# A hybrid diffusion layer on one core: three modulation blocks move to the vector engine in operations of 1024 columns, and the output product adds two row blocks in PSUM

## Chip, cores and metric

The kernel runs on one core of a Trainium2 chip. The metric is the device time of one execution in microseconds, here the median of several runs. Engines have the short names of the profile: PE (TensorE, matmuls), PEld (its weight loads), DVE (VectorE), ACT (ScalarE), POOL (GpSimd), SP (SyncE, which issues the weight transfers). Each engine works through its own list of instructions strictly in order, so an instruction that waits holds up all that stand behind it on its engine.

## What is computed

One layer with a gated short convolution as token mixer and a mixture of 16 experts; 256 tokens, 2048 channels, all in float32. Cut to what matters here:

```python
mod = split(silu(c) @ mod_w + mod_b, 6)            # six rows of 2048; mod_w is 2048 x 12288
h = x * (1 + mod[1]) + mod[0]
gate_b, gate_c, val = split(h @ w_in, 3)           # w_in is 2048 x 6144
o = (gate_b * depthwise_conv3(gate_c * val)) @ w_out
x = layer_norm(ALPHA * x + mod[2] * o)
h2 = x * (1 + mod[4]) + mod[3]                     # goes to the router and the experts
x = layer_norm(ALPHA * x + mod[5] * hier_moe(h2))  # top 1 of 4 groups, top 2 of its 4 experts
```

Each of the six `mod` rows is a product of one vector of 2048 with a 2048 x 2048 block of weights: 16 MB are read for very little arithmetic.

## The kernel before, in words

All weights are read once, as a stream of loads of up to 1.5 MB in a fixed order (`steps`, line 564 on). A load goes into one of six places of a ring (`get`, line 118) and is issued by SP when the instructions that used the place's former tenant are done. The part up to the router, which the change touches, runs like this:

- **Input product** (`cin_step`, line 390). The weights `w_in` are cut into eight groups of channels. The first four groups are worked through in five passes over the contraction (`acc_step`, line 442: passes `i` = 0 to 4, each adding to sums in SBUF, `acc`), because the rows of `mod[0]` and `mod[1]` that `h` needs come in only pass by pass. The last four groups (`full_steps`, line 453) accumulate in PSUM over four steps of one load each. A step has three splits of 1024 columns (`split`, line 376): ACT rounds the weights to `hic` (line 379), DVE subtracts to get the rest `loc` (line 380), and PE multiplies three products of these pieces with the pieces of `h` (lines 387 to 389), 24 matmuls of 256 columns for a split. There are two buffers each for `hic` and `loc`: ACT's next rounding waits until PE is through with the split before last.
- **Convolution** (`conv_group`, line 415) of a group once its sums are complete: six DVE operations and two of ACT, ending in `yh` and `yl`.
- **Output product** (`cout_step`, line 506): 16 steps of 512 rows (`qt`) by 512 columns (`j`), each with two splits (`hio`, `loo`) and 24 matmuls of 512 columns. Each of the 16 adds its own result to the residual: DVE multiplies it by `mod[2]` (line 531), and DVE (`qt` 0 and 3) or POOL (`qt` 1 and 2, line 535) adds it to `xt`.
- **Modulation.** `mod[0]`, `mod[1]`, `mod[2]` and three eighths of `mod[3]` and `mod[4]` are multiplied on PE, with the weights as moving columns, in four partitions' quarters (lines 258 and 285). The other five quarters of `mod[3]` and `mod[4]` (`ON_V`) go to DVE: 15 operations of 512 columns each (line 263), which `gemv_cols` puts into a `queue`; each `split` takes two of them off the queue behind its own subtraction.

DVE's list is therefore a mixture of subtractions, for which PE waits, and of queued multiplications, which nobody waits for until the block is complete. After the last output step come the layer norm's statistics (lines 538 and 637), the router and the sixteen experts, which read 302 MB of weights and are not touched by the change.

Of the kernel before, what the change touches and what calls it, by code (L numbers as in the profile page):

```python
# [19 lines left out]
P = 128  # L20
D = 2048
# [12 lines left out]
EXTRA = [0, 1, 0, 0, 12]  # L34
# [16 lines left out]
# Pieces of the columns of the down product; those of the last experts end with smaller ones.  # L51
# [14 lines left out]
def trunk_kernel(  # L66
# [36 lines left out]
    # ---------------------------------------------------------------- weight stream  # L103
# [14 lines left out]
    def get(i):  # L118
        """the tile of load i, whose predecessors have been used; issues what now has a place"""
# [24 lines left out]
    def expert_loads(e, pieces=QUARTERS):  # L144
        """loads of an expert's gate and up weights, and of its down weights by pieces of the columns"""
# [19 lines left out]
    # ---------------------------------------------------------------- constants, small inputs  # L165
# [10 lines left out]
    # picks rows 0, 32, 64 and 96  # L176
# [38 lines left out]
    # arithmetic that waits for its turn on the tensor engine, and on the vector engine  # L215
# [10 lines left out]
    def gemv_cols(m, c0, n, on_vector=False):  # L226
# [3 lines left out]
        nb, k0 = n // P, c0 // P  # L230

        def late():
            pt = aux_tile(f"gc{m}_{c0}")
            for i in range(nb):
                TE.transpose(pt[:, i * P : (i + 1) * P], box["r"][:, i * P : (i + 1) * P], ident)
# [999 lines left out]
```

## Time and profile before

| what | value |
|---|---|
| median of 3 runs | 1348.4 us (1347.04 to 1348.72) |
| profiled execution, span from first to last instruction | 1343.3 us; the page gives no other time of it, and the median is 5.1 us above it |
| PE busy | 1190.9 us (89%) |
| DVE busy | 724.2 us (54%) |
| ACT busy | 404.6 us (30%) |
| POOL busy | 30.3 us (2%) |
| transfers | 475.85 MB, mean 354 GB/s |

Busy is the time in which at least one instruction of an engine ran. A matmul's end is modelled and later than the start of the next one, so PE's pace is read from the distance of starts in the timeline, not from a duration. Of float32 matmuls two records stand in the trace for one in the program. [...]

### The profile page before, as it was taken

What the parts mean: (1) busy time and instruction counts of PE and PEld (TensorE: products, weight loads), DVE (VectorE), ACT (ScalarE), POOL (GpSimd) and SP (SyncE); (2) the same over time, 40 slices, a digit from 0 to 9 for tenths busy, and PEclk for the clock granted to TensorE, in tenths of its full rate; (3) what the DMA queues carried; (4) which work ended last, traced back from release to release, by engine and by line L of the source; (5) the groups of instructions that cost most, each with busy time, mean ns of one, the idle gap of its engine ahead of it and who ended that gap; (6) DMA issues with size and microseconds to landing.
All of it is one profiled execution on the core that took longest, in us unless ns stands there. A gap on an engine that the chain in (4) does not pass through costs nothing. (4 is left out here: it accounts for less than half of the span.)

```text
span 1343.3 us, 23490 instructions
## 1 busy us (share of the span) xinstructions
PE 1190.9 (89%) x9429; PEld 856.0 (64%) x9429; DVE 724.2 (54%) x1526; ACT 404.6 (30%) x795; POOL 30.3 (2%) x60
## 2 busy tenths in 40 slices
PE   4999999999999999998789878997689888898883
PEld 2778876978699875775367446774267454554553
DVE  2665565597789878686266434583147321122217
ACT  1333333434244334563035223451026110100020
POOL 0000000000400120000000000000000000000000
PEclk7999999999999999999889899998789899999996
DMA  9999879799989879979999899989999999999992
GB/s 321 354 396 395 298 279 398 276 310 351 357 312 337 296 280 342 364 263 365 413 414 347 316 414 411 400 304 381 412 412 393 336 412 412 413 371 414 412 410 78
DMA packets 240947, 475.85 MB, mean 354 GB/s; under 512 B 10968, under 2 KB 74680, under 8 KB 240576
## 3 DMA queue, kind: packets, MB, share of 16 engines
q1 hardware_dynamic: 235808, 471.88, 93.2%
q10 hardware_dynamic: 5024, 2.40, 0.6%
q8 instruction: 76, 1.25, 0.3%
q14 instruction: 39, 0.32, 0.1%
HBM read 472.16 MB, written 2.10 MB: 353 GB/s over the span
## 5 line engine op out<-in xcount | busy, mean ns | idle before, releaser
L904 PE MATMUL gue<-w,xgp 128*32 128x384 f32 (+1 forms) x1536 | 218.1, 554 | 71.2 <-DMA w<-in_ex_w_up_dram 59.0
L387 PE MATMUL ci<-hhi,hic 128*128 128x256 f32 x768 | 221.1, 289 | 2.7 <-ACT hic L379 1.4
L389 PE MATMUL ci<-hhi,loc 128*128 128x256 f32 x768 | 218.6, 286 | 3.6 <-DVE loc L380 3.5
L388 PE MATMUL ci<-hlo,hic 128*128 128x256 f32 x768 | 217.9, 284 | 0.8 <-DVE hlo L374 0.7
L904 PEld LDWEIGHTS gue<-w,xgp 128*32 128x32 f32 (+1 forms) x1536 | 83.1, 130 | 197.8 <-issue 83.0
L693 DVE TENSOR_TENSOR parts<-w,parts 128x256 fp32r<-128x256 f32 (+1 forms) x320 | 135.3, 475 | 73.2 <-ACT parts L692 70.4
L692 ACT CAST parts<-w 128x256 fp32r<-128x256 f32 (+1 forms) x320 | 131.3, 449 | 114.5 <-PE gue L901 72.7
L379 ACT CAST hic<-w 128x1024 fp32r<-128x1024 f32 (+1 forms) x108 | 102.5, 954 | 183.2 <-PE ci L388 159.0
L387 PEld LDWEIGHTS ci<-hhi,hic 128*128 128x128 f32 x768 | 145.1, 189 | 14.9 <-issue 8.4
L389 PEld LDWEIGHTS ci<-hhi,loc 128*128 128x128 f32 x768 | 145.2, 190 | 9.5 <-DVE loc L380 6.0
L388 PEld LDWEIGHTS ci<-hlo,hic 128*128 128x128 f32 x768 | 146.4, 191 | 5.6 <-DVE hlo L374 2.5
L380 DVE TENSOR_TENSOR loc<-w,hic 128x1024 fp32r<-128x1024 f32 (+1 forms) x108 | 118.7, 1108 | 35.2 <-ACT hic L379 35.0
L921 ACT COPY gse<-gue 128x384 f32<-128x384 f32 x16 | 7.7, 480 | 314.8 <-PE gue L904 314.8
L904 PE MATMUL gue<-w,xfp 128*128 128x384 f32 x256 | 93.9, 498 | 2.5 <-DMA w<-in_ex_w_gate_dram 2.5
L1014 DVE TENSOR_TENSOR Y<-dne,m 32x128 f32<-32x128 f32 (+2 forms) x176 | 52.6, 299 | 42.3 <-PE dne L947 39.3
L448 DVE TENSOR_TENSOR acc<-acc,ci 128x512 f32<-128x512 f32 x48 | 33.0, 687 | 60.4 <-PE ci L389 60.4
L822 PE MATMUL gap<-ohp,xt 128*128 128x128 f32 x512 | 63.6, 279 | 1.7 <-DVE xtp L837 1.0
L822 PEld LDWEIGHTS gap<-ohp,xt 128*128 128x128 f32 x512 | 59.5, 192 | 8.7 <-issue 4.2
L258 PE MATMUL gv<-w,sT 128*32 128x512 f32 (+1 forms) x416 | 57.6, 569 | 8.2 <-DMA w<-in_mod_w_dram 8.2
L904 PEld LDWEIGHTS gue<-w,xfp 128*128 128x128 f32 x256 | 48.3, 194 | 23.5 <-issue 3.9
L263 DVE SCALAR_TENSOR_TENSOR rows<-w,sT,rows 128x512 f32<-128x512 f32 x75 | 57.9, 773 | 1.3
L954 PE MATMUL dne<-parts,ahe 128*128 128x256 f32 x192 | 57.6, 300 | 0.3 <-DVE parts L693 0.2
(302 smaller groups left out, 1679.8 us busy)
## 6 DMA issues: line engine op xcount, KB each, us to landing
w<-in_ex_w_gate_dram SPq DMA_DIRECT2D x64, 1536.0 KB, 13.6
w<-in_ex_w_up_dram SPq DMA_DIRECT2D x64, 1536.0 KB, 15.6
w<-in_ex_w_down_dram SPq DMA_DIRECT2D x60, 1536.0 KB, 15.0
w<-in_mod_w_dram SPq DMA_DIRECT2D x48, 1536.0 KB, 9.3
w<-in_conv_in_w_dram SPq DMA_DIRECT2D x84, 512.0 KB, 6.9
w<-in_mod_w_dram SPq DMA_DIRECT2D x22, 1024.0 KB, 8.0
w<-in_conv_out_w_dram SPq DMA_DIRECT2D x16, 1024.0 KB, 6.9
w<-in_conv_in_w_dram SPq DMA_DIRECT2D x24, 256.0 KB, 7.2
```

Of the source, the lines that this page charges most:

```text
L258: TE.matmul(box["ps"][32 * g : 32 * g + 32, :n], sT[:, kt : kt + 1].to_broadcast([P, 32]), ws, start=kt < 4, stop=kt >= 12)
L263: V.scalar_tensor_tensor(out=box["r"][:, :n], in0=ws, scalar=sT[:, kt : kt + 1], in1=box["r"][:, :n], op0=ALU.mult, op1=ALU.add)
L379: S.copy(hi[:, :n], src)
L380: V.tensor_sub(lo[:, :n], src, hi[:, :n].bitcast(F32))
L387: TE.matmul(ps, whi, ahi, start=start, stop=False)
L388: TE.matmul(ps, whi, alo, start=False, stop=False)
L389: TE.matmul(ps, wlo, ahi, start=False, stop=stop)
L692: S.copy(hi[:, :n], src)
L693: V.tensor_sub(lo[:, :n], src, hi[:, :n].bitcast(F32))
L822: TE.matmul(ps[:, k * n : (k + 1) * n], xn[:, h, (k0 + k) * P : (k0 + k + 1) * P], oh[:, h, :n], start=h == 0, stop=h == 1)
L904: TE.matmul(dst, big[0][:, KF.index(kt), :] if cc == 128 else xg[:, kt, :cc], src, start=st_, stop=sp_)
L954: TE.matmul(o, a[i], lo[:, :256], start=False, stop=sp_ and m == 1)
```

## The change

`mod[2]`, `mod[3]` and `mod[4]` are multiplied on DVE as a whole, in six halves of 1024 columns: one ACT multiplication and 15 DVE operations of 1024 columns for a half. Their loads are blocks of 3 x 128 rows by 1024 columns. Each `split` takes one queued operation, or two when more than three are queued. Each half's sums over partitions come from eight small products with a column of ones (`col_sums`), instead of transposes and a reduction; for `mod[2]` from two products with ones of 512 columns (`mod2_rows`). Three of the loads now stand in pass 3 and eight in pass 4 (`EXTRA`); the rest stand between the later steps.

The output product runs over pairs of row blocks: `qt` 0 and 1 (then 2 and 3) accumulate in one pair of PSUM tiles, so the multiplication by `mod[2]` and the addition to `xt` happen 8 times instead of 16, and POOL adds nothing any more. The first half of the product stands in one block of eight steps behind the second step of group 4, after a flush of the queue; the second half stands at the end. Two things move from DVE to ACT: the unrounded `h` (line 373) and the copies of pass 0 (line 446).

```diff
-EXTRA = [0, 1, 0, 0, 12]
+EXTRA = [0, 1, 0, 3, 8]
-VN = 2
-ON_V = [[0, 1, 0, 1], [0, 1, 1, 1]]
+WIDE = 1024
...
+    def col_sums(m, c0, n, rows_, ones_):
+        pt, nb, k0 = aux_tile(f"gc{m}_{c0}"), n // P, c0 // P
+        for i in range(nb):
+            TE.matmul(pt[:, i : i + 1], rows_[:, i * P : (i + 1) * P], ones_, start=True, stop=True)
+        V.scalar_tensor_tensor(
+            out=modT[:, m, k0 : k0 + nb], in0=pt[:, :nb], scalar=1.0 if m in (1, 4) else 0.0,
+            in1=modbT[:, m * KT + k0 : m * KT + k0 + nb], op0=ALU.add, op1=ALU.add)
...
+    def gemv_vector(m, c0, done):
+        box = {}
+        per = 3072 // WIDE
+        for t0 in range(0, KT, per):
+            nt = min(per, KT - t0)
+            def work(w, t0=t0, nt=nt):
+                for k in range(nt):
+                    kt = t0 + k
+                    ws = w[:, k * WIDE : (k + 1) * WIDE]
+                    if kt == 0:
+                        box["r"] = mod2b[:, c0 : c0 + WIDE] if m == 2 else big_tile(f"rows{m}{c0}")[:, :WIDE]
+                        S.mul(box["r"], ws, sT[:, kt : kt + 1])
+                        continue
+                    def fn(ws=ws, kt=kt):
+                        V.scalar_tensor_tensor(out=box["r"], in0=ws, scalar=sT[:, kt : kt + 1], in1=box["r"],
+                                               op0=ALU.mult, op1=ALU.add)
+                        if kt == KT - 1:
+                            pending.append(lambda: done(box["r"]))
+                    queue.append(fn)
+            yield mod_load(m, c0, WIDE, t0, nt), work
...
+    def mod2_rows(c0, r):
+        for i in range(WIDE // 512):
+            q = c0 // 512 + i
+            rq, o = r[:, i * 512 : (i + 1) * 512], slice(32 * q, 32 * q + 32)
+            V.tensor_tensor(out=rq[o], in0=rq[o], in1=bias_rows[2][o], op=ALU.add)
+            ps = aux_tile(f"gb2{q}")
+            TE.matmul(ps[:, :], onesF.to_broadcast([P, P]), rq, start=True, stop=True)
+            S.copy(mod2b[:, q * 512 : (q + 1) * 512], ps[:, :])
...
-                V.tensor_scalar(out=ht, in0=src, scalar1=sc, scalar2=sh, op0=ALU.mult, op1=ALU.add)
+                S.activation(ht, src, AF.Identity, bias=sh, scale=sc)
...
-        for fn in queue[:VN]:
-            fn()
-        del queue[:VN]
+        drain(2 if len(queue) > 3 else 1)
...
-                    V.tensor_copy(accs[g][:, a, :], pss[a][:, :])
+                    S.copy(accs[g][:, a, :], pss[a][:, :])
...
+    def cout_steps(half):
+        out = []
+        for j in range(4):
+            pso = []
+            for qt in (2 * half, 2 * half + 1):
...
+                def work(w, qt=qt, j=j, pso=pso):
+                    if qt % 2 == 0:
+                        pso.extend(mm_tile(f"co{half}{j}{h}") for h in range(2))
...
+                                first, last = (qt % 2, pr, k) == (0, 0, 0), (qt % 2, pr, k) == (1, 1, 1)
+                                TE.matmul(pso[h][:, :], yh[:, k, a:b], wh, start=first, stop=False)
+                                TE.matmul(pso[h][:, :], yl[:, k, a:b], wh, start=False, stop=False)
+                                TE.matmul(pso[h][:, :], yh[:, k, a:b], wl, start=False, stop=last)
+                    if qt % 2 == 0:
+                        return
...
-                elif qt < 3:
-                    G.tensor_tensor(out=xs, in0=xs, in1=tmp, op=ALU.add)
...
-        if g < 6:
-            rest += fs[:2] + qt + fs[2:]
-        elif g == 6:
-            rest += fs
-        else:
-            rest += fs + qt_last
+        if g == ACC_GROUPS:
+            fs = fs[:2] + [(None, lambda w: flush())] + cout_steps(0) + fs[2:]
+        rest += fs
```

What the scheduler makes of it on DVE is seen at three places. In the rows, `loc_GA` and `loo` are the subtractions of a split (G the group, A the split), `acc` the additions of a pass, `mod2b` and `rows` the sums of a modulation block, `t` the multiplication by `mod[2]`, `x3` three instructions of the kind in a row.

DVE in pass 3, between the splits of group 2 and of group 3, before:

```order
L380 TENSOR_TENSOR loc_22_1674<-w_1472,hic_22_1673 128x1024
L448 TENSOR_TENSOR acc_185<-acc_185,ci_21_1615 128x512
L448 TENSOR_TENSOR acc_185<-acc_185,ci_22_1616 128x512
L380 TENSOR_TENSOR loc_30_1726<-w_1583,hic_30_1725 128x1024
L380 TENSOR_TENSOR loc_31_1754<-w_1583,hic_31_1753 128x1024
```

and now:

```order
L470 TENSOR_TENSOR acc_185<-acc_185,ci_21_1609 128x512
L275 SCALAR_TENSOR_TENSOR mod2b<-w_1479,sT,mod2b 128x1024 x2
L470 TENSOR_TENSOR acc_185<-acc_185,ci_22_1610 128x512
L275 SCALAR_TENSOR_TENSOR mod2b<-w_1479,sT,mod2b 128x1024
L275 SCALAR_TENSOR_TENSOR mod2b<-w_1577,sT,mod2b 128x1024 x3
L275 SCALAR_TENSOR_TENSOR mod2b<-w_1586,sT,mod2b 128x1024 x3
L404 TENSOR_TENSOR loc_30_1718<-w_1594,hic_30_1717 128x1024
L404 TENSOR_TENSOR loc_31_1748<-w_1594,hic_31_1747 128x1024
```

The flush ahead of the next pass puts nine multiplications between two subtractions that stood two additions apart.

DVE in the first half of the output product, before:

```order
L380 TENSOR_TENSOR loo_2736<-w_2617,hio_2735 128x1024
L531 TENSOR_TENSOR t_2721<-co_2683,mod2b 128x512
L531 TENSOR_TENSOR t_2724<-co_2684,mod2b 128x512
L533 SCALAR_TENSOR_TENSOR xt<-xt,t_2721 128x512
L533 SCALAR_TENSOR_TENSOR xt<-xt,t_2724 128x512
L263 SCALAR_TENSOR_TENSOR rows_2679<-w_2481,sT,rows_2679 128x512
L380 TENSOR_TENSOR loo_2754<-w_2617,hio_2753 128x1024
```

and now:

```order
L404 TENSOR_TENSOR loo_2718<-w_2596,hio_2717 128x1024
L275 SCALAR_TENSOR_TENSOR rows_2681<-w_2594,sT,rows_2681 128x1024
L275 SCALAR_TENSOR_TENSOR rows_2681<-w_2635,sT,rows_2681 128x1024 x3
L404 TENSOR_TENSOR loo_2739<-w_2637,hio_2738 128x1024
L404 TENSOR_TENSOR loo_2757<-w_2637,hio_2756 128x1024
L275 SCALAR_TENSOR_TENSOR rows_2681<-w_2679,sT,rows_2681 128x1024 x2
L561 TENSOR_TENSOR t_2773<-co_2697,mod2b 128x512
```

Up to four wide multiplications stand between two pairs of subtractions.

DVE between groups 4 and 5, now:

```order
L404 TENSOR_TENSOR loc_52_3150<-w_2869,hic_52_3149 128x1024
L453 TENSOR_TENSOR v_3070<-v_3070,ci_40_2314 128x512
L275 SCALAR_TENSOR_TENSOR rows_2964<-w_2873,sT,rows_2964 128x1024
L457 TENSOR_TENSOR yl_3079<-v_3070,yh_3078 128x512
L275 SCALAR_TENSOR_TENSOR rows_2964<-w_2873,sT,rows_2964 128x1024 x2
L275 SCALAR_TENSOR_TENSOR rows_2964<-w_2962,sT,rows_2964 128x1024 x2
L404 TENSOR_TENSOR loc_50_3187<-w_2976,hic_50_3186 128x1024
```

Five wide multiplications and two operations of the convolution stand between two subtractions here; before, the same two had one operation of the convolution between them.

## Rows read from the trace of the kernel before

**Rows 1.** Busy time of each engine in stretches of 25 us; the first line names the columns.

```profile
core 0: us, PE busy (x) PEld busy (x) DVE busy (x) ACT busy (x) POOL busy (x), PEclk, DMA share, GB/s
...
400.00:425.00 25.00, 24.75 (x206) 24.54 (x206) 23.62 (x32) 11.10 (x13) 0.00 (x0) 1.00 0.98 352
...
650.00:675.00 25.00, 17.18 (x182) 8.93 (x176) 3.14 (x11) 2.88 (x8) 0.00 (x0) 0.86 1.04 412
...
950.00:975.00 25.00, 16.32 (x189) 6.73 (x181) 4.50 (x18) 1.30 (x4) 0.00 (x0) 0.80 1.04 411
```

**Rows 2.** The same for three longer stretches up to the router.

```profile
165.00:250.00 85.00, 80.58 (x617) 61.50 (x616) 54.19 (x79) 31.57 (x43) 0.00 (x0) 1.00 0.94 347
250.00:450.00 200.00, 196.85 (x1415) 174.19 (x1414) 161.30 (x199) 76.50 (x84) 13.52 (x8) 1.00 0.90 314
450.00:513.00 63.00, 61.06 (x309) 42.24 (x311) 50.21 (x72) 20.66 (x24) 13.40 (x8) 1.00 0.82 294
```

**Rows 3.** DVE's and ACT's lists near 427 us: start, duration, engine, line, tiles, count.

```profile
426.35 1.53 DVE L263 SCALAR_TENSOR_TENSOR rows<-w,sT,rows 128x512 f32<-128x512 f32 x2
...
427.00 1.05 ACT L379 CAST hic<-w 128x1024 fp32r<-128x1024 f32 x1 [1.21 <-PE ci L388]
...
429.88 1.05 ACT L379 CAST hic<-w 128x1024 fp32r<-128x1024 f32 x1 [1.83 <-PE ci L388]
```

**Rows 4.** ACT's list in the output product.

```profile
478.62 1.05 ACT L379 CAST hio<-w 128x1024 fp32r<-128x1024 f32 x1 [1.67 <-PE co L525]
481.34 1.05 ACT L379 CAST hio<-w 128x1024 fp32r<-128x1024 f32 x1 [1.67 <-PE co L525]
```

**Rows 5.** Groups of instructions up to 520 us: count, busy us, mean ns, idle time before.

```profile
L380 DVE TENSOR_TENSOR loc<-w,hic 128x1024 fp32r<-128x1024 f32 x84 | 102.7, 1228 | 30.6 <-ACT hic L379 30.4
...
L263 DVE SCALAR_TENSOR_TENSOR rows<-w,sT,rows 128x512 f32<-128x512 f32 x75 | 57.9, 773 | 1.3
...
L258 PE MATMUL gv<-w,sT 128*32 128x512 f32 x288 | 44.4, 599 | 0.0
L380 DVE TENSOR_TENSOR loo<-w,hio 128x1024 fp32r<-128x1024 f32 x32 | 41.9, 1313 | 15.4 <-ACT hio L379 15.3
L285 PE MATMUL gv<-w,sT 128*32 128x512 f32 x230 | 34.0, 596 | 0.0
...
L535 POOL TENSOR_TENSOR xt<-xt,t 128x512 f32<-128x512 f32 x16 | 26.9, 1704 | 451.5 <-DVE t L531 451.5
...
L531 DVE TENSOR_TENSOR t<-co,mod2b 128x512 f32<-128x512 f32 x32 | 21.4, 687 | 2.7 <-PE co L525 2.4 <-PE lps L501 0.2
L380 DVE TENSOR_TENSOR loc<-w,hic 128x512 fp32r<-128x512 f32 x24 | 16.0, 686 | 4.6 <-ACT hic L379 4.6
...
L235 PE MATMUL gc<-ident,rows 128*128 128x128 f32 x64 | 10.5, 282 | 0.5 <-ACT rows L270 0.5
L371 ACT ACTIVATE hhi<-xT,modT 128x256 fp32r<-128x256 f32 x16 | 9.0, 564 | 9.9 <-DVE ht L373 5.6 <-PE xT L366 2.3 <-DVE modT L239 2.0
```

**Rows 6.** The experts' gather products, from the same view of the whole span.

```profile
L822 PE MATMUL gap<-ohp,xt 128*128 128x128 f32 x512 | 63.6, 279 | 1.7 <-DVE xtp L837 1.0 <-DVE xgp L790 0.7
```

**Rows 7.** DVE's list: pass 3, a convolution, the first step of group 4, the layer norm.

```profile
164.75 0.69 DVE L448 TENSOR_TENSOR acc<-acc,ci 128x512 f32<-128x512 f32 x1 [3.88 <-PE ci L389]
...
246.12 0.69 DVE L420 TENSOR_TENSOR u<-acc 128x512 f32<-128x512 f32 x1
246.73 1.22 DVE L380 TENSOR_TENSOR loc<-w,hic 128x1024 fp32r<-128x1024 f32 x1
247.86 0.88 DVE L426 SCALAR_TENSOR_TENSOR v<-u,T2t,v 128x255 f32<-128x255 f32 x2
...
249.44 1.22 DVE L380 TENSOR_TENSOR loc<-w,hic 128x1024 fp32r<-128x1024 f32 x1
...
512.59 0.38 DVE L637 BATCH_NORM_AGGREGATE mv<-stats 128x2 f32<-128x24 f32 x2
```

**Rows 8.** The input product's matmuls: count, shortest, median and longest, first and last start.

```profile
L387 PE MATMUL ci<-hhi,hic x768: 274/282/684, 27.8 to 450.0; 128*128 128x256 f32 x192
```

More of the change, by code (lines that the diff above doesn't have):

```diff
@@ L248, in work @@
                 if t0 == 0:
[L249 to L252 removed]
+                    box["ps"] = aux_tile(f"gv{m}_{c0}")
                 for k in range(nt):
@@ L268, in work @@
-                if t0 + nt == KT and not on_vector:
-                    box["r"] = p1.tile([P, 512], F32, tag="rows", bufs=2, name=f"rows{m}{c0}")
-                    S.copy(box["r"][:, :n], box["ps"][:, :n])
-                    pending.append(late)
-            yield mod_load(m, c0, n, t0, nt), work
+                    TE.matmul(box["ps"][32 * g : 32 * g + 32, :n], sT[:, kt : kt + 1].to_broadcast([P, 32]),
+                              w[:, k * n : (k + 1) * n], start=kt < 4, stop=kt >= 12)
@@ L372, in make_h, with drain @@
                 ht = p1.tile([P, T], F32, tag="e", bufs=3, name=f"ht{kt}")
-                V.tensor_scalar(out=ht, in0=src, scalar1=sc, scalar2=sh, op0=ALU.mult, op1=ALU.add)
+                S.activation(ht, src, AF.Identity, bias=sh, scale=sc)
                 V.tensor_sub(hlo[:, kt, :], ht, hhi[:, kt, :].bitcast(F32))
+    def drain(n):
+        for fn in queue[:n]:
+            fn()
+        del queue[:n]
     def split(src, n, name):
@@ new lines, in cout_steps, with load @@
+    def cout_steps(half):
[3 more added lines that the diff above has]
+            for qt in (2 * half, 2 * half + 1):
+                def load(w, qt=qt, j=j):
+                    nc.sync.dma_start(
+                        w[:, :2048].rearrange("p (t c) -> p t c", c=512),
+                        rows(cout[qt * 512 : (qt + 1) * 512, j * 512 : (j + 1) * 512]),
+                    )
+                def work(w, qt=qt, j=j, pso=pso):
+                    if qt % 2 == 0:
+                        pso.extend(mm_tile(f"co{half}{j}{h}") for h in range(2))
+                    for pr in range(2):
+                        hi, lo = split(w[:, pr * 1024 : (pr + 1) * 1024], 1024, f"o{qt}{j}{pr}")
+                        yh, yl = yhi[qt * 2 + pr], ylo[qt * 2 + pr]
+                        for k in range(2):
+                            for h in range(2):
+                                a, b = h * P, (h + 1) * P
+                                wh, wl = hi[:, k * 512 : (k + 1) * 512], lo[:, k * 512 : (k + 1) * 512]
+                                first, last = (qt % 2, pr, k) == (0, 0, 0), (qt % 2, pr, k) == (1, 1, 1)
[4 more added lines that the diff above has]
+                        return
+                    if half and j > 0:
+                        router_part(j - 1)
+                    for h in range(2):
+                        xs = xt[:, h, j * 512 : (j + 1) * 512]
+                        tmp = p1.tile([P, 512], F32, tag="e", bufs=3, name=f"t{half}{j}{h}")
+                        V.tensor_mul(tmp, pso[h][:, :], mod2b[:, j * 512 : (j + 1) * 512])
+                        if half == 0:
+                            V.scalar_tensor_tensor(out=xs, in0=xs, scalar=ALPHA, in1=tmp, op0=ALU.mult, op1=ALU.add)
+                        else:
+                            V.tensor_add(xs, xs, tmp)
+                            V.bn_stats(stats[:, h, j, :], xs)
+                    if half and j == 3:
+                        router_part(3)
+                out.append((load, work))
+        return out
@@ L587, in trunk_kernel @@
     steps = h_mods(0) + [(None, lambda w: h_hook(0)())]
-    late = [st for m in (2, 3, 4) for q in range(4) for st in mods(m, q)]
+    late = [st for m in (2, 3, 4) for q in range(D // WIDE) for st in mods(m, q)]
     last = [st for q in range(4) for st in mods(5, q)]
```

76 lines of the change are left out of this document (9 added, 67 removed).

## Prediction, made before the changed kernel was run

> **What bounds the kernel now.** I began with the busy times by stretches, since the change ends where the router begins. From 165 to 450 us PE is busy all but 7.6 of 285 us, at the full granted clock; DVE is at 64% and then at 81%, and the transfers keep a share of 0.94 and 0.90 [rows 2]. So up to the router the kernel hangs on PE. Later stretches, among the experts, look different: there the transfers run at 1.04 and PE waits [rows 1]; whatever happens ahead of them shifts them as a whole, because at the router the transfers have slack already (0.82) [rows 2].
>
> Next comes PE's pace. ACT's roundings of an input product's splits start 2.88 us apart where nothing disturbs [rows 3]; that is 24 matmuls at 0.12 us. In the output product they start 2.72 us apart [rows 4]. Within such a beat DVE has one subtraction (next start 1.13 us later [rows 7]) and two queued multiplications of 512 columns (1.53 us [rows 3]): 2.66 of 2.88 us. It fits, barely: from 400 to 425 us DVE is busy 23.6 of 25 us, PE 24.75 [rows 1]. The reader should see that DVE is the second engine at its limit, not a free one.
>
> **The change, part by part.**
>
> *PE loses work.* `mod[2]` had 64 products, 128 records at 34.0 / 230 = 0.148 us: 18.9 us. The three PE quarters of `mod[3]` and `mod[4]` had 48, 96 records at 44.4 / 288 = 0.154 us: 14.8 us [rows 5]. The transposes for sums (32 at 10.5 / 64 = 0.164 us, 5.2 us [rows 5]) become 32 one-column products; bounds are the transpose's 0.164 and a 128-column product's two records, 2 x 63.6 / 512 = 0.25 us [rows 6]. I take 0.25, so +2.8 us. In all PE loses 31 us.
>
> *DVE gains work.* 75 operations of 512 columns become 90 of 1024; 88 of them come after 165 us. No wide one is in the trace. Below it is bounded by the narrow one, 0.77 us, above by two, 1.55 us [rows 5]. The subtraction of the same operand kinds grows from 0.686 to 1.228 us when its columns double [rows 5], so 0.773 + 0.542 = 1.31 us lone and, with the overlap to a neighbour seen in the lists, 1.28 us. That is 113 us for 88 where 58 us stood. The 16 dropped multiplications by `mod[2]` give back 16 x 0.6 = 10 us. Net DVE gets some 45 us more, in a part where it had 81% already.
>
> *Cost nothing:* the unrounded `h` (16 operations like ACT's at 0.56 us [rows 5]) and 12 copies on ACT: ACT is busy 31.6 of 85 us [rows 2], and without that cover it would be 16 us. POOL's 16 additions (1.70 us each) lay beside; what they cost is that DVE's subtractions there took 1.313 instead of 1.228 us, 32 x 0.085 = 2.7 us [rows 5], which I keep in the range. The transfers' bytes and their count (36 loads for the three blocks) stay; the most crowded part below needs about 25 MB in 74 us, 340 GB/s, and 412 is seen [rows 1].
>
> Now the sum, by the order of DVE's list. Operations are taken by distance of starts: subtraction 1.14, wide multiplication 1.28, addition or other operation of 512 columns 0.63, `t` and what follows it 0.60, a convolution 3.5 (u, two pairs of 0.8, two more of 0.63) [rows 7].
>
> 1. *Up to the addition of pass 3, group 2,* at 165 us [rows 7]: unchanged, limits as before.
> 2. *To the end of the first step of group 4.* Before: 165 to 250.6 us [rows 7], PE-bound. Now DVE has 27 wide (34.6), 18 subtractions (20.5), 16 additions (10.1), four convolutions (14.0), two biases (1.3): 80.5 us, PE some 67. About 4.5 us are added where an addition of pass 4 waits for PE's split. End: 250, as before, although PE has 17 us less to do: what PE is spared DVE takes.
> 3. *The first half of the output product with its surroundings:* 31 wide (39.7), 19 subtractions (21.7), 12 operations on results (7.2), two biases (1.3): 69.9 us, PE about 57. Twice or three times `t` waits for PE's second split, 4 us in all. End: 324.
> 4. *Ten steps of groups 4 to 6:* 30 subtractions (34.2), 30 wide (38.4), three convolutions (10.5), 2.4 more: 85.5 us. PE has 30 x 2.88 = 86.4 and 6 us of one-column products. Here neither hides the other well, since the list is lumpy: five wide multiplications and two other operations between two subtractions make 8.8 us while PE has 3.1 us left to do; PE stands 5.7 us. By the same count it stands 1.4 us behind three wide ones, about 7.4 us ahead of group 7 (three wide, one more, the last convolution), and 2 us in small pieces. 86.4 + 16.5 + some 2 of the products that fall into no gap = 105 us. End: 429.
> 5. *Group 7 and the second half:* 12 splits, 34.6 us, then eight output steps as before, from 450.0 [rows 8] to 512.6 [rows 7], 62.6 us. End: 526.
>
> Before, the statistics came at 512.6; the sum says 526.0, **13.4 us later**. The profiled span 1343.3 becomes 1356.7, and the runs' median lay 5.1 us above that span: **1361.8, so 1362 us**, 1.0% slower. Both ends of the wide operation's price would move the sum far (88 x -0.5 or +0.25 us); the range rests on 1.28 with some 0.1 either way.
>
> [...]
>
> **The rivals.**
>
> *DVE packs densely.* The waits of parts 2 to 4 don't arise, because PE and ACT are always ahead of a busy DVE. Then 165 + 80.5 + 69.9 + 92 (PE in part 4) + 97.2 = 504.6, 8 us earlier than before: 1340 us, faster. For it: before, DVE at 94% and PE at full pace lived side by side for 25 us [rows 1]. Against it: there the queue came two narrow operations at a time, evenly. It decides if the added waits are below 13 us; I count 22.
>
> *The clock falls.* PE would have 124 us of work in the 159 us of parts 2 and 3, a share of 0.78; the stretch with 17.2 of 25 us was granted 0.86 [rows 1]. At 0.86, 28% of 159 us would be at half pace, 22 us of PE's work lost; PE has 35 us to spare there, but in the wrong places. Half of it, 11 us, would come on top: 1373 us. Against it: PE's gaps here are shorter and split by bursts of several us.
>
> *PE's relief counts in full,* DVE being no bound: 31 us and more, 1318 us. The DVE sums speak against it: no part can be shorter than DVE's own work.
>
> **How the numbers follow.** Forecast 0.55, dense packing 0.22, falling clock 0.19, PE's relief 0.04. The time is the forecast's. The range takes in dense packing with the 2.7 us of POOL's stretching (1338) and the falling clock with a little for loads that come late because a ring place waits for a queued multiplication (1377). About 0.2%, 2.7 us, is what a measurement of this kernel can tell from none. Faster by more: most of dense packing and PE's relief, 0.23. Within: the waits at half of what I count, 0.13. Slower: 0.64.
>
> **What would show it.** Right: DVE busy around 95% from 165 to 430 us; PE's count of input matmuls per 25 us clearly under the 206 of before [rows 1] in passes 3 and 4; the wide operation at about 1.3 us; PE released by `loc` and `loo` in the waits; group 7's last matmul some 13 us after 450; the experts' part as long as before. Wrong, if PE still runs without gaps from 165 to 450 us, if the wide operation takes 1.0 us or less, or if the statistics come before 512 us.

## The result: 3.6% slower, and where the time went

The changed kernel took 1395.0 us in the median of 4 runs (1393.4 to 1395.8); the kernel before, beside it, 1347.7 us. The ratio is 1.0358, 95% interval 1.0339 to 1.0377: 47 us lost, where 13.4 were predicted and the range ended at 1377. The profiled execution took 1393.4 us with a span of 1391.7.

First the stretches of the changed kernel that answer to [rows 1, 2] (columns: length, busy us of each engine with its instructions, granted clock, share of the transfers, GB/s; the clock is a share of PE's full speed, and the traces of both kernels hold two values of it, 1.00 and 0.50):

```profile
165.00:250.00 85.00, 62.32 (x430) 57.42 (x423) 70.97 (x84) 29.06 (x39) 0.00 (x0) 0.84 0.79 283
200.00:342.00 142.00, 119.57 (x671) 102.41 (x670) 134.00 (x146) 47.21 (x55) 0.00 (x0) 0.90 0.84 309
250.00:450.00 200.00, 178.05 (x1184) 162.68 (x1183) 174.08 (x180) 69.17 (x75) 0.00 (x0) 0.93 0.94 334
450.00:513.00 63.00, 63.00 (x419) 54.17 (x419) 36.10 (x43) 24.27 (x26) 0.00 (x0) 1.00 0.63 220
650.00:675.00 25.00, 18.78 (x299) 14.26 (x295) 19.61 (x43) 0.98 (x3) 0.00 (x0) 1.00 1.04 395
950.00:975.00 25.00, 19.52 (x339) 14.54 (x339) 12.75 (x46) 5.82 (x15) 0.00 (x0) 0.90 1.05 385
```

Two different things stand here. From 165 to 342 us PE has gaps, its clock is at 0.84 and 0.90 on the mean (before: 1.00), and DVE is busy 134 of 142 us. But look at the last two lines too: among the experts, where the program is unchanged, the transfers are as busy as before (1.04 and 1.05) and move 395 and 385 GB/s instead of 412 and 411 [rows 1]. The same share of time carries 4 and 6% less.

Then DVE's list, with the places of [rows 7]:

```profile
172.42 0.68 DVE L470 TENSOR_TENSOR acc<-acc,ci 128x512 f32<-128x512 f32 x1
...
178.66 9.20 DVE L275 SCALAR_TENSOR_TENSOR mod2b<-w,sT,mod2b 128x1024 f32<-128x1024 f32 x7
187.78 2.35 DVE L404 TENSOR_TENSOR loc<-w,hic 128x1024 fp32r<-128x1024 f32 x2
...
263.06 1.22 DVE L404 TENSOR_TENSOR loc<-w,hic 128x1024 fp32r<-128x1024 f32 x1
...
339.83 1.29 DVE L563 SCALAR_TENSOR_TENSOR xt<-xt,t 128x512 f32<-128x512 f32 x2
...
540.82 0.38 DVE L660 BATCH_NORM_AGGREGATE mv<-stats 128x2 f32<-128x24 f32 x2
```

These are the ends of parts 1, 2, 3 and 5 of the prediction: 172.4 us (165 predicted), 264.3 (250), 341.1 (324) and 540.8 (526). In lengths: part 1 is 7.4 us longer than said, part 2 91.9 instead of 85, part 3 76.8 instead of 74, parts 4 and 5 199.7 instead of 202. The statistics start 28.2 us later than the 512.6 of before, 14.8 more than predicted. From there to the end the changed kernel takes 1391.7 - 540.8 = 850.9 us, the kernel before 830.7: 20.2 us that the prediction did not have at all.

The prices of single operations were right. Groups up to 520 us, as [rows 5]:

```profile
L275 DVE SCALAR_TENSOR_TENSOR rows<-w,sT,rows 128x1024 f32<-128x1024 f32 x60 | 76.8, 1282 | 0.9
L275 DVE SCALAR_TENSOR_TENSOR mod2b<-w,sT,mod2b 128x1024 f32<-128x1024 f32 x30 | 38.4, 1281 | 0.9 <-ACT mod2b L271 0.6
L404 DVE TENSOR_TENSOR loo<-w,hio 128x1024 fp32r<-128x1024 f32 x28 | 33.9, 1221 | 15.1 <-ACT hio L403 15.1
```

The wide multiplication took 1.28 us, as chosen, and without POOL's additions the subtraction in the output product fell from 1.313 to 1.221 us. PE's waits up to 545 us (in total, times, longest):

```profile
PE ci L411 <- DVE loc L404: 24.9, 15, 9.8
PE ci L409 <- ACT hic L403: 14.3, 8, 4.5
PE co L553 <- DVE loo L404: 8.2, 3, 3.8
```

PE is released by `loc` and `loo`, as predicted, but for 14.3 us also by ACT's `hic`; the longest wait is the one behind the seven multiplications at 178.66. It ends at 189.05 us, and the product of `hhi` and `hic` next in PE's list starts at 189.43, though ACT was done with that `hic` by 178.66. Parts 2 and 3 as stretches, and what DVE waited for in part 2 and, in the last of these fences, in part 3:

```profile
172.40:264.30 91.90, 67.23 (x459) 62.29 (x457) 81.66 (x97) 29.83 (x38) 0.00 (x0) 0.85 0.76 265
264.30:341.10 76.80, 68.43 (x324) 55.79 (x325) 72.76 (x71) 23.54 (x24) 0.00 (x0) 0.91 0.98 364
```

```profile
DVE acc L470 <- PE ci L411: 9.0, 5, 4.0
```

```profile
DVE loo L404 <- ACT hio L403: 2.7, 3, 1.2
```

All runs in one table. "Statistics" is the start of the layer norm's statistics in the profiled execution, "rest" the span behind it; "ring" is the byte of each SBUF partition at which the weight ring starts. The ratio of a run is to the kernel before as it ran beside it (medians 1345.7 to 1347.7 us). e11 leaves out most of the modulation's products and the router picks otherwise: its time and its rest can't be compared with the others.

| kernel | ring | median us | ratio, 95% interval | statistics | rest |
|---|---|---|---|---|---|
| before | 98816 | 1347.7 | | 512.6 | 830.7 |
| changed | 98752 | 1395.0 | 1.0339 to 1.0377 | 540.8 | 850.9 |
| e1 | 98816 | 1378.1 | 1.0207 to 1.0266 | 543.6 | 832.5 |
| e2 | 98752 | 1366.8 | 1.0118 to 1.0176 | 511.7 | 854.0 |
| e3 | 98816 | 1355.9 | 1.0051 to 1.0098 | 523.2 | 833.2 |
| e4 | 98816 | 1370.1 | 1.0153 to 1.0213 | 536.9 | 829.6 |
| e5 | 98816 | 1357.0 | 1.0056 to 1.0102 | 524.2 | 831.4 |
| e6 | 98816 | 1379.2 | 1.0210 to 1.0263 | 542.8 | 834.8 |
| e7 | 98816 | 1376.1 | 1.0187 to 1.0244 | 542.0 | 831.2 |
| e8 | 98816 | 1351.8 | 1.0026 to 1.0055 | 518.9 | 832.9 |
| e9 | 98816 | 1375.2 | 1.0186 to 1.0239 | 542.7 | 830.5 |
| e10 | 98816 | 1379.8 | 1.0217 to 1.0282 | 546.6 | 832.3 |
| e11 | 98816 | 1346.4 | 0.9983 to 1.0022 | 513.7 | 829.8 |
| e12 | 98816 | 1368.0 | 1.0135 to 1.0188 | 533.7 | 835.5 |
| e13 | 98304 | 1346.8 | 0.9987 to 1.0007 | 511.8 | 833.0 |
| e14 | 98944 | 1363.4 | 1.0103 to 1.0140 | 510.8 | 851.3 |
| e15 | 99072 | 1346.7 | 0.9992 to 1.0015 | 511.3 | 834.8 |
| e16 | 98816 | 1376.7 | 1.0202 to 1.0250 | 542.8 | 832.5 |
| e17 | 98816 | 1342.5 | 0.9965 to 0.9992 | 507.4 | 835.4 |
| e18 | 98816 | 1357.7 | 1.0058 to 1.0098 | 516.9 | 839.9 |

### The profile page after: what moved, and what is told of

The parts are those of the page before. It is cut to its first block, busy times and chain, and to the rows that moved or that the text cites. A ratio compares the mean times of both kernels' runs of the same rounds, so it can differ in the third digit from the quotient of the medians.

```text
span 1391.7 us, 23127 instructions
## 1 busy us (share of the span) xinstructions
PE 1183.0 (85%) x9269; PEld 874.5 (63%) x9269; DVE 742.8 (53%) x1475; ACT 416.4 (30%) x817; POOL 3.3 (0%) x44
## 5 line engine op out<-in xcount | busy, mean ns | idle before, releaser
L927 PE MATMUL gue<-w,xgp 128*32 128x384 f32 (+1 forms) x1536 | 223.7, 567 | 84.3 <-DMA w<-in_ex_w_up_dram 70.4
L411 PE MATMUL ci<-hhi,loc 128*128 128x256 f32 x768 | 224.8, 294 | 25.3 <-DVE loc L404 24.9
L409 PE MATMUL ci<-hhi,hic 128*128 128x256 f32 x768 | 224.9, 293 | 14.9 <-ACT hic L403 14.3
L410 PE MATMUL ci<-hlo,hic 128*128 128x256 f32 x768 | 221.8, 289 | 0.1
L411 PEld LDWEIGHTS ci<-hhi,loc 128*128 128x128 f32 x768 | 151.3, 198 | 30.4 <-DVE loc L404 29.9
L409 PEld LDWEIGHTS ci<-hhi,hic 128*128 128x128 f32 x768 | 151.9, 198 | 21.8 <-ACT hic L403 17.1
L410 PEld LDWEIGHTS ci<-hlo,hic 128*128 128x128 f32 x768 | 151.8, 198 | 0.7 <-DVE hlo L392 0.4
L275 DVE SCALAR_TENSOR_TENSOR rows<-w,sT,rows 128x1024 f32<-128x1024 f32 x60 | 76.8, 1282 | 0.9
L553 PE MATMUL co<-loo,yh 128*128 128x512 f32 x128 | 52.4, 419 | 8.3 <-DVE loo L404 8.2
L977 PE MATMUL dne<-parts,ahe 128*128 128x256 f32 x192 | 58.1, 303 | 0.3 <-DVE parts L716 0.2
L975 PE MATMUL dne<-parts,ahe 128*128 128x256 f32 x192 | 58.0, 302 | 0.0
```

The lines of the kernel that those rows point to most:

```text
L275: V.scalar_tensor_tensor(out=box["r"], in0=ws, scalar=sT[:, kt : kt + 1], in1=box["r"], op0=ALU.mult, op1=ALU.add)
L409: TE.matmul(ps, whi, ahi, start=start, stop=False)
L410: TE.matmul(ps, whi, alo, start=False, stop=False)
L411: TE.matmul(ps, wlo, ahi, start=False, stop=stop)
L927: TE.matmul(dst, big[0][:, KF.index(kt), :] if cc == 128 else xg[:, kt, :cc], src, start=st_, stop=sp_)
L975: TE.matmul(o, a[i], hi[:, :256], start=st_ and m == 0, stop=False)
```

## Experiments on the place of the weight ring

The change drops `sm`, two tiles for sums (tag `gsum`), from the pool `const`, which lies ahead of the pool `ring` in SBUF. With them 64 bytes go, and all six places of the ring move from 98816 (193 x 512) to 98752 (1543 x 64). Nothing else in the experts' part differs, so that was the first suspect.

**e1**, the changed kernel with the 64 bytes put back:

```diff
     mod2b = p1.tile([P, D], F32, name="mod2b")
+    pad = const.tile([P, 16], F32, name="pad")
```

> The changed kernel with 64 bytes of unused constant put ahead of the weight ring, so that the ring's six places start at byte 98816 of each partition (193 x 512) as before the change, not at 98752. Theory (placement: the removed 64 bytes of sums moved the ring off a multiple of 512 bytes and every weight transfer became about 4% slower): the experts' stretches move 411 to 416 GB/s again instead of 393 to 399, statistics to end takes about 831 us instead of 851, the subtractions near 165 us come 0 to 3 us behind the kernel before instead of 8, and the time falls to 1360 to 1372 us. Rival (the lower rate comes from the wide modulation loads or from the chip, not from the place): 1390 to 1398 us, 395 GB/s.

**e2**, the kernel before with the ring moved:

```diff
-            sm = const.tile([P, 4], F32, tag="gsum", bufs=2, name=f"gs{m}_{c0}")
+            sm = p1.tile([P, 4], F32, tag="gsum", bufs=2, name=f"gs{m}_{c0}")
```

> The kernel before with its 64 bytes of sums taken from the pool behind the ring instead of the one ahead of it: same instructions, the ring at 98752 instead of 98816. Theory (placement): 393 to 399 GB/s among the experts, statistics to end about 851 us, a few us more ahead of 165 us, 1368 to 1380 us in all. Rival: 1345 to 1350 us, 412 GB/s.

The same stretch as the last but one above, first of e1, then of e2:

```profile
650.00:675.00 25.00, 20.46 (x324) 15.08 (x325) 22.23 (x47) 1.57 (x4) 0.00 (x0) 1.00 1.04 412
```

```profile
650.00:675.00 25.00, 17.15 (x156) 7.53 (x149) 1.65 (x6) 1.33 (x4) 0.00 (x0) 0.80 1.04 393
```

Both ways the rate goes with the place: 412 with the ring at 98816, 393 at 98752. e1 gains 17 us over the changed kernel, e2 loses 20 us, and the rest behind the statistics is 832.5 and 854.0 us. One half of both expectations missed, and with it their ranges (e1 took 1378.1 us instead of 1360 to 1372, e2 1366.8 instead of 1368 to 1380): up to the router nothing came back in e1 (543.6, not earlier), and e2 loses nothing there (511.7). In these kernels the place costs only behind the statistics, where the transfers' share from 650 to 675 us is 1.04; up to the router (0.91 from 70 to 520 us in the kernel before) no cost shows.

**e13, e14, e15** ask which boundary counts, all in the kernel before: e13 by the first of these edits, e14 by the second, e15 by the same with 64 for 32:

```diff
-    T1 = const.tile([P, P], F32, name="T1")
+    T1 = p1.tile([P, P], F32, name="T1")
...
+    pad = const.tile([P, 32], F32, name="pad")
```

> The kernel before with a 512-byte tile of the start (T1) taken from the pool ahead of the ring to the one behind it: the ring at 98304 = 48 x 2048 instead of 98816 = 193 x 512. Theory (a multiple of 512 is what counts): same, 1343 to 1350 us, 411 to 416 GB/s among the experts. Rival (the larger the power of two, the faster): 1325 to 1340 us, over 418 GB/s.

> The kernel before with 128 unused bytes ahead of the ring: 98944, a multiple of 128 but not of 256. Theory (a multiple of 512 is what counts): as e2_before_ring_off_512, 1362 to 1370 us, 393 to 399 GB/s among the experts. Rival (a multiple of 128 is enough, 98752 is one of 64 only): 1343 to 1350 us.

> The kernel before with 256 unused bytes ahead of the ring: 99072, a multiple of 256 but not of 512. Theory (a multiple of 512): 1362 to 1370 us. Rival (256 or less is enough): 1343 to 1350 us.

e13 and e15 are as fast as before (833.0 and 834.8 us behind the statistics), e14 is slow (851.3). From 650 to 675 us e13 and e15 move 411 GB/s, e14 moves 393. So of the starts tried those at a multiple of 256 are enough, 98944 at one of 128 is not, and 2048 buys nothing more; the 512 of my theory was wrong by a factor of two. The transfers' own view shows it per packet: packets, MB, share of 16 engines' span, for the kernel before and for e2.

```profile
q1 hardware_dynamic: 235808, 471.88, 93.2%
```

```profile
q1 hardware_dynamic: 235808, 471.88, 95.0%
```

The same packets take 0.932 x 1343.3 x 16 / 235808 = 0.0849 us each, and 0.950 x 1365.7 x 16 / 235808 = 0.0880 us off the boundary, 3.6% more. Here the reading end never moved and the writing end did; by what a packet takes longer, no run shows.

## Experiments on the loss up to the router

**e3 and e4** take the two halves of the change apart. e3 is the kernel before with `cout_steps`, without the flush; e4 is e1 with the old `cout_step`:

```diff
-        qt = [cout_step(g - 4, j) for j in range(4)] if 4 <= g < 7 else []
...
+        if g == ACC_GROUPS:
+            fs = fs[:2] + cout_steps(0) + fs[2:]
```

> The kernel before with the paired output product alone (two row blocks in PSUM, no additions on POOL), modulation as before, ring at 98816. Theory (the loss up to the router comes from the list of VectorE, which the wide multiplications fill): VectorE loses 10 us of multiplications by mod[2] and the stretching of its subtractions, TensorE's work stays, so 1338 to 1348 us. Rival (the pairs are what costs: PSUM places held for two steps, output product crowded into groups 4 and the end): over 1350 us.

> The changed kernel with the output product of before (one row block each, additions on POOL), wide modulation on VectorE kept, ring at 98816. Theory (VectorE's list sets the pace up to the router): VectorE has some 10 us more to do than in the changed kernel with the ring at 98816, so 2 to 12 us slower than that run: 1365 to 1382 us. Rival (the paired output product is what costs): 1340 to 1352 us.

The pairs alone cost 8.7 us (e3), as its rival had it, and without them the wide modulation costs 22.9 (e4), against 30.9 for both (e1). The costs add up. e4's range came, but not its reason: it was to be 2 to 12 us slower than e1, and it is 8.0 us faster. "Pairs" here takes in the place of the steps, since e3 also moves the first half of the output product into one block. A loss can be read in e3's lists, first DVE's, then PE's:

```profile
304.74 0.69 DVE L539 TENSOR_TENSOR t<-co,mod2b 128x512 f32<-128x512 f32 x1 [2.45 <-PE co L531]
...
308.48 2.35 DVE L380 TENSOR_TENSOR loo<-w,hio 128x1024 fp32r<-128x1024 f32 x2
310.75 5.47 DVE L263 SCALAR_TENSOR_TENSOR rows<-w,sT,rows 128x512 f32<-128x512 f32 x7
```

```profile
305.68 0.39 PE L529 MATMUL co<-hio,yh 128*128 128x512 f32 x1
305.91 0.40 PE L530 MATMUL co<-hio,yl 128*128 128x512 f32 x1
309.75 1.22 PE L531 MATMUL co<-loo,yh 128*128 128x512 f32 x2 [3.44 <-DVE loo L380]
...
311.19 0.63 PE L530 MATMUL co<-hio,yl 128*128 128x512 f32 x1
311.62 0.63 PE L531 MATMUL co<-loo,yh 128*128 128x512 f32 x1
```

DVE stands 2.45 us at `t` until PE has the pair's second block; the next pair's `loo` stands behind it in the list, and PE stands 3.44 us for it. After that the matmuls start 0.43 us apart instead of 0.23; in the changed kernel such products start 0.43 us apart at a granted clock of 0.50 (312 to 316 us) and 0.23 us apart at 1.00 (317 to 320 us). What the gap costs by its length and what by the slow products behind it, no run separates. A second one lies at 419 to 425 us, behind the convolution of group 6.

**e5** wanted to remove the first wait by writing what DVE does with a pair's results behind the next pair's first split:

```diff
+                    held.append(results)
+                    if j == 3:
+                        held.pop()()
...
+                        if held:
+                            held.pop()()
```

> The paired output product alone, as in e3_paired_output_product_only, but what VectorE does with a pair's results is written behind the first split of the next pair. [...]

It changed nothing (1357.0 us, where the author had 1347 to 1353 if this wait was the cost and 1354 to 1360 if the crowding of the steps was): the gap is still there, 2.84 us at 308.65, since `t` and the multiplications still surround `loo` in DVE's list. The order of the list isn't simply that of the text. The second range was met, but that the crowding is the cause has not been shown.

**e6** lets the end of a pass run the pending sums alone and leaves the queue:

```diff
-            flush()
+            old = pending[:]
+            pending.clear()
+            for f in old:
+                f()
```

> The changed kernel with the ring at 98816, where the end of a pass no longer empties the queue of multiplications but leaves it to the splits. Theory (the lump of seven wide multiplications is a gap of 9.8 us and a stretch at the low clock, but VectorE has the same work to do by 340 us): the wait of 9.8 us near 181 us is gone, the first half of the output product still ends within 5 us of 342.3, 1371 to 1379 us. Rival (lumps are what costs, VectorE's sum is not): 10 us or more faster than e1_after_ring_at_512's 1378, under 1368 us.

```profile
179.73 9.20 DVE L275 SCALAR_TENSOR_TENSOR mod2b<-w,sT,mod2b 128x1024 f32<-128x1024 f32 x7
```

The lump of seven is still there, and so is the time, 1379.2: the flush did not make it, though the section on the change puts the multiplications there down to it. The run says nothing on what the lump costs.

**e9** puts idle products into PE's gaps instead (`fill`, called ahead of the first products of a step), to see what the low clock costs:

```diff
+    def fill(ps, us):
+        for _ in range(round(us / 0.12)):
+            TE.matmul(ps[:, :T], hhi[:, 0, :P], hhi[:, 0, :], start=True, stop=True)
...
+                if first:
+                    fill(pss[a], FILL.get((k0, g, a), 0))
...
```

> The changed kernel with the ring at 98816 and idle products (256 columns, overwritten later) put on TensorE where it stood: 4.0, 9.8, 3.8 and 5.8 us at the ends of passes and in the last pass, 2.2, 3.8 and 2.2 us at the pairs, 5.4 us in group 5; nothing else changes. [...] Rival (VectorE's list alone sets the times, the clock costs nothing): 1376 to 1384 us.

From 200 to 342 us, e1 and e9:

```profile
200.00:342.00 142.00, 119.77 (x669) 102.60 (x669) 133.19 (x145) 47.70 (x54) 0.00 (x0) 0.90 0.83 309
```

```profile
200.00:342.00 142.00, 136.25 (x912) 123.54 (x911) 134.73 (x147) 48.86 (x55) 0.00 (x0) 0.99 0.85 312
```

In this stretch the clock is back at 0.99 and PE is busy 136 of 142 us, yet the last addition of the first half of the output product starts at 341.9 us instead of 342.3. (From here on the end of that half is read at this start; the 341.1 above is the end of that addition in the changed kernel.) The total falls by 2.9 us, not by the 4 to 14 that the author gave if the low clock was half of the loss up to the router (1364 to 1374 us), and lies between this range and the rival's; against the kernel before beside each it is 1.5 us. So from 200 to 342 us, where DVE is busy 94%, holding the clock up brought nothing that can be told from the scatter; whether the idle products themselves held up real ones was not separated.

But the test leaves out the longest gap. `fill` stands ahead of the `hic` products of a step, and PE stands behind them, for `loc`; e9's wait there is still 9.5 us:

```profile
PE ci L411 <- DVE loc L404: 13.3, 7, 9.5
```

Behind that gap e1 works at the low level, 0.50, and DVE has to wait for it (first the clock from 190 to 195 us, then DVE's list):

```profile
190.00:195.00 5.00, 4.19 (x19) 4.19 (x20) 1.90 (x2) 0.00 (x0) 0.00 (x0) 0.50 1.02 386
```

```profile
195.82 0.69 DVE L471 TENSOR_TENSOR acc<-acc,ci 128x512 f32<-128x512 f32 x1 [3.92 <-PE ci L411]
```

In e9 DVE waits 3.3 us at the same place. Of 61 us at the low level from 70 to 520 us, 31 were left (0.97 on the mean instead of 0.93), more than the 25 that the author had reckoned with. What the low clock costs in part 2 is therefore open.

**e11** takes the multiplications' length away and leaves their number and order:

```diff
-                        V.scalar_tensor_tensor(out=box["r"], in0=ws, scalar=sT[:, kt : kt + 1], in1=box["r"],
-                                               op0=ALU.mult, op1=ALU.add)
+                        V.scalar_tensor_tensor(out=box["r"][:, :32], in0=ws[:, :32], scalar=sT[:, kt : kt + 1],
+                                               in1=box["r"][:, :32], op0=ALU.mult, op1=ALU.add)
```

> The changed kernel with the ring at 98816, whose wide multiplications take 32 of the 1024 columns; the products of the other columns are left out after the first row, so the modulation, and what the router picks, are others. To be read up to the statistics alone. Theory (VectorE is the bound from 165 to 342 us): the first half of the output product ends 12 to 25 us earlier than 342.3, TensorE stands less than 20 us of 450 instead of 52, the statistics come at 505 to 522 us instead of 543.6. Rival (transfers, casts on ScalarE or the pairs are the bound): statistics at 530 us or later.

The statistics in e11:

```profile
513.73 0.38 DVE L661 BATCH_NORM_AGGREGATE mv<-stats 128x2 f32<-128x24 f32 x2
```

The products of the other 992 columns are left out, so the run is read up to the statistics alone. They come 29.9 us earlier than in e1, and the first half of the output product ends 20.9 us earlier, at 321.4. So the time of the multiplications on DVE is worth 30 us. The second reading is as useful: even with DVE nearly rid of them, the kernel reaches the router 1.1 us later than before. The 31 us of work that PE lost are eaten by other gaps and by a lower clock, 0.95 on the mean instead of 1.00 (PE still stands 34.6 of the 450 us from 70 to 520, not under 20 as expected; before 11.2). Among the gaps are 4.0 us at 84 us and 4.6 at 219 behind ACT's casts, 5.3 at 236 behind the bias of `mod[2]` on DVE and 4.4 at 418 behind `loc`.

**e16** cuts each wide multiplication into two of 512 columns, one behind the other:

```diff
+                        for o in (slice(0, 512), slice(512, 1024)):
+                            V.scalar_tensor_tensor(out=box["r"][:, o], in0=ws[:, o], scalar=sT[:, kt : kt + 1],
+                                                   in1=box["r"][:, o], op0=ALU.mult, op1=ALU.add)
```

> The changed kernel with the ring at 98816, each wide multiplication done as two of 512 columns, one behind the other: VectorE has 88 x (1.55 - 1.28) = some 24 us more to do up to the router, in smaller pieces. Theory (VectorE's total is the bound from 165 to 342 us): the first half of the output product ends 8 to 20 us behind 342.3, 1388 to 1402 us. Rival (the size of the pieces is what makes TensorE stand): 1365 to 1380 us.

```profile
200.00:342.00 142.00, 119.86 (x681) 102.52 (x681) 138.94 (x196) 47.56 (x54) 0.00 (x0) 0.92 0.85 314
```

My price was off (the narrow ones took 0.75 us, not 0.77, so DVE had 8 us more from 70 to 520, not 24), and DVE is now at 98%; but the first half ends at 340.9 us, not later, and the total, 1376.7, is e1's within the scatter. That lies in the rival's range, but so does e1's own 1378.1. Neither theory holds as it stood: more time on DVE in finer pieces cost nothing, and finer pieces gained nothing clear. DVE's total alone is not the bound: it stood 8.8 of the 142 us in e1 and stands 3.1 here, so the pieces used up idle time.

**e7 and e10** test what made part 1 late, e7 by the first of these edits to e1, e10 by the second:

```diff
-                S.activation(ht, src, AF.Identity, bias=sh, scale=sc)
+                V.tensor_scalar(out=ht, in0=src, scalar1=sc, scalar2=sh, op0=ALU.mult, op1=ALU.add)
...
-EXTRA = [0, 1, 0, 3, 8]
+EXTRA = [0, 1, 0, 0, 11]
```

> The changed kernel with the ring at 98816 and the unrounded h computed by VectorE as before the change, instead of by ScalarE. Theory (at the end of a pass ScalarE makes each h twice, and the next casts stand behind that, so TensorE waits 4.0 us near 81 us and the clock falls): that wait is under 3 us, the subtractions at 110 to 165 us lie 2 to 6 us behind the kernel before instead of 5 to 11, and 1370 to 1377 us. Rival (VectorE bounds everything, so giving it 16 operations back costs): 1380 to 1386 us.

> The changed kernel with the ring at 98816 and the loads for the three blocks spread over the passes as before the change (1 in pass 1, the others in the last pass) instead of 3 in pass 3 and 8 in the last. Theory (the 3 loads, 4.7 MB, some 11 us of transfers in pass 3, make that pass late, and VectorE, being the bound afterwards, never gets that back): the additions at the end of pass 3 come some 5 us earlier than e1_after_ring_at_512's 174.2 us, and 1370 to 1376 us. Rival (VectorE's multiplications only start later then and the sum stays): 1376 to 1382 us.

The addition that ends part 1, in e1 and in e10:

```profile
174.18 0.68 DVE L471 TENSOR_TENSOR acc<-acc,ci 128x512 f32<-128x512 f32 x1
```

```profile
168.88 0.69 DVE L471 TENSOR_TENSOR acc<-acc,ci 128x512 f32<-128x512 f32 x1 [1.68 <-PE ci L411]
```

The three loads in pass 3 cost 5.3 us there. But in e10 the first half of the output product ends at 344.1 us and the total is 1379.8, in the rival's range: what is won in pass 3 is lost in pass 4, where DVE then has its work later. In e7 the addition stands at 172.1, the wait near 81 us shrinks from 4.0 to 2.9 us, the end of that half moves by 1.6 us and the total by 2.0. That is no more than runs differ in which `h` stays on ACT (172.4 in the changed kernel, 173.5 in e6, 174.2 in e1), so no price of the second `h` on ACT beyond the 1.1 us of the wait is shown.

## Experiments on a better mixture

**e8** is the kernel before with six quarters in halves of 1024 on DVE (one behind each split) and the other six on PE; **e12** moves the second half of `mod[2]` too.

```diff
-VN = 2
+VN = 1
...
-        return list(gemv_cols(m, q * 512, 512, ON_V[m - 3][q]))
+        if m == 3 and q < 2:
+            return list(gemv_cols(m, q * 512, 512))
+        c0 = q * 512
+        return list(gemv_vector(m, c0, lambda r: col_sums(m, c0, WIDE, r, onesF))) if q % 2 == 0 else []
```

> The kernel before, with block 3's second half and all of block 4 multiplied 1024 columns at a time on VectorE (48 wide operations, 61 us) instead of five quarters of 512 (80 narrow, 62 us); block 2 and the first half of block 3 stay on TensorE, one wide operation follows a split. Theory (TensorE is the bound up to the router and VectorE keeps up if its list is even): TensorE loses one quarter, about 5 us, and the transposes of six sums; the statistics come 2 to 6 us ahead of 512.6, 1341 to 1346 us. Rival (a list with wide operations makes TensorE wait): 1348 to 1356 us.

> As e8_halves_of_3_and_4_wide, and the second half of block 2 on VectorE too (16 wide operations, 20 us, in the last pass, where VectorE was at 64%). Theory: TensorE loses 9.4 us more, VectorE has room, so 1334 to 1344 us. Rival (VectorE becomes the bound in the last pass as in the changed kernel, TensorE's gaps bring the low clock): 1346 to 1356 us.

e8 is in its rival's range with 1351.8 us; e12, at 1368.0, is 12 us above the end of its rival's. e12 shows the changed kernel's trouble in small: from 200 to 342 us PE is busy 122.3 us at a clock of 0.92.

**e17** goes the other way, one more quarter on DVE in narrow operations. **e18** takes only the one-column products for the sums, with the 64 bytes kept. Both are edits to the kernel before:

```diff
-ON_V = [[0, 1, 0, 1], [0, 1, 1, 1]]
+ON_V = [[0, 1, 1, 1], [0, 1, 1, 1]]
...
-                TE.transpose(pt[:, i * P : (i + 1) * P], box["r"][:, i * P : (i + 1) * P], ident)
+                TE.matmul(pt[:, i : i + 1], box["r"][:, i * P : (i + 1) * P], onesF if on_vector else selG, start=True, stop=True)
...
```

> The kernel before with quarter 2 of block 3 on VectorE too, 512 columns an operation: TensorE loses 32 records of 0.154 us, about 5 us, VectorE gains 16 x 0.77 = 12 us between 250 and 450 us, where it was at 81%. Theory (TensorE is the bound and VectorE in small pieces keeps up): 1340 to 1346 us. Rival (VectorE is already where its list makes TensorE wait): 1348 to 1356 us.

> The kernel before with the sums into columns done by one-column products instead of transposes and reductions, nothing else. Theory (the smallest part of the change is worth what TensorE and VectorE save at the places where they are the bound, 1 to 2 us): 1343 to 1348 us. Rival (the products are longer than the transposes, 0.25 us against 0.16): 1348 to 1352 us.

```profile
507.44 0.38 DVE L637 BATCH_NORM_AGGREGATE mv<-stats 128x2 f32<-128x24 f32 x2
```

In e17 the statistics come 5.2 us ahead of before, what PE was relieved of, and the total is 1342.5 us, as its theory had it, ratio 0.9979 (0.9965 to 0.9992): the only version faster than both kernels, by some 3 us. e18, at 1357.7, is above both its ranges: the statistics come 4.3 us late and the rest takes 839.9 us. Among the experts it moves the full 413 GB/s from 650 to 675 us; in the 80 us that begin 40 us behind the statistics, the router's stretch, it moves 289 and 293 (two halves) instead of 310 and 307. Why the small products cost that stays open. e8, e12 and the changed kernel have them too, so neither e8's loss nor the changed kernel's 23 us can be put to the wide operations alone.

## Why the prediction was wrong, point by point

- *"The experts' part as long as before"* failed, and was the largest miss: 20.2 of the 35 us between the sum's 1356.7 and the span of 1391.7. The sum followed instructions and never asked where the tiles would lie. e1, e2, e14 and e15 show it: the ring at 98752 or 98944, no multiples of 256 bytes, costs 16 to 20 us against 98816 or 99072.
- *Part 1, "unchanged, limits as before"*, failed by 7.4 us. The prediction counted the three loads moved to pass 3 as bytes that stay; e10 puts 5.3 us on them, and its addition at 168.9 is still 4.1 us later than the 164.75 of before [rows 7], for reasons that stay open. ACT's second `h`, counted as hidden, shows in one wait near 81 us, of which e7 takes 1.1 us. What is won in part 1 did not come back at the end in e10.
- *Part 2* was 6.9 us too short. DVE's own work was 81.7 us busy, near the 80.5 counted; the term that was too small is the wait of pass 4's additions for PE, 9.0 us instead of 4.5. Its longest piece, 4.0 us, comes behind the seven multiplications in a row, for which PE had waited 9.8 us.
- *Part 3* was 2.8 us too short in DVE's own work: 72.8 us busy instead of 69.9, with 21 subtractions and 16 operations on results where 19 and 12 were counted. The 4 us of idle time came, but behind ACT's roundings (3.4 us) and not at `t` (0.2 us): the size was luck.
- *Parts 4 and 5*, 202 us, came out at 199.7. The gap of 5.7 us behind five wide multiplications came as 5.4.
- *The wide multiplication at 1.28 us* and the count of 88 were right. That the relief of PE is worth nothing as long as DVE is behind was right too, and in e11, with DVE out of the way, it brought nothing either.
- *The pairs*, of which the sum took only relief, cost 8 to 9 us (e3 against before, e1 against e4). That DVE's list waits for two row blocks instead of one is seen in e3; how much of the loss that is, and how much the crowding of the steps, is not shown.
- *From span to time.* The 5.1 us added at the end compared one execution with the median of others. The changed kernel's 1393.4 us lies 1.7 us above the span of the same execution; by that, the profiled execution of before was the fastest one (1344.9 us), and some 3.4 us of the forecast were scatter.
- *The rivals.* Dense packing did not come: PE's waits for `loc`, `hic` and `loo` up to 545 us add up to 47.4 us, against the 13 from which it decides. The clock fell about as the rival said (0.85 in part 2 and 0.91 in part 3, where it took 0.86), but its price is not shown: e9 halves the time at the low level and gains at most 2.9 us, and leaves out the longest gap. Behind that gap of 9.8 us the granted clock of e1 was 0.50 (190 to 195 us). The half pace at the low level was the author's estimate: in the changed kernel products of 256 columns start 0.213 us apart at 0.50 and 0.119 at 1.00, 1.8 times as far.
- *Of what was to show it*: DVE at 95% came only from 200 to 342 us (94%), not up to 430 (87% from 250 to 450). The last matmul of group 7 came at 477.9 us, 28 us behind 450 and not 13.

In sum, of 47 us: about 17 from the ring's place, 8 from the pairs, 23 from the wide modulation and what was moved with it. Up to the router e1 is 31.0 us behind the kernel before, and without the time of the multiplications on DVE (e11) 29.9 of them go. What the small products, the loads and ACT's new work have in the 23 is not told apart.

## What to carry to other kernels

When a change touches a small tile, see where the large buffers behind it then start; compare the rate of transfers in a part that was not edited before explaining anything else, and try the buffers' start at a multiple of 256 bytes, with which the rate here was 411 or 412 GB/s instead of 393 (from 650 to 675 us). Work moved to a second engine stands in the same list as the operations that the first one waits for, and how much fits there is found by steps: one quarter more paid 3 us (e17), while the changed kernel's modulation cost 23. That shorter pieces help is not shown: cutting the wide ones (e16) gained nothing clear. Before a fallen clock is called the cost, fill the gaps with idle products and see whether the time follows, and see too whether the longest gap was filled.

## What was not expected of the hardware

Transfers into SBUF slowed by 3.6% a packet (0.0849 to 0.0880 us; 412 to 393 GB/s) when their places started 192 bytes past a multiple of 256, and e14, with 128 bytes past, lost nearly as much (393 GB/s). The busy share of the transfer engines among the experts was 1.04 with either place: the share alone hides it. After a gap of 3.44 us products of 512 columns started 0.43 us apart instead of 0.23; keeping PE busy with idle products held the clock at 0.99 instead of 0.90 from 200 to 342 us without making that stretch faster.
